# One core of Trainium2, a two-layer hybrid backbone: the last feed-forward by seven half-size products, and four pieces of work moved in the streams before it

## The chip, the cores and the metric

The kernel runs on one core of one Trainium2 chip. The core has a matrix engine (PE, with its weight loads listed apart as PEld), a vector engine (DVE), a scalar engine (ACT), a general one (POOL), and queues that move data between the chip's memory and the core (their issues are listed under SP). Each engine works through its own list of instructions in order and waits there for what others must deliver. The metric is the time of one execution on the device in microseconds (us), and one kernel's time is the median of several runs.

## What is computed

Two layers over 512 latent tokens and 256 context tokens with 1024 features. Each layer is a half-step feed-forward, a mixing step (attention with grouped heads, a short gated convolution, attention with compressed queries and keys), and a second half-step feed-forward. The context leaves the net after the mixing step of the second layer, so the last of the four feed-forwards has 512 tokens and the other three have 768.

```
def rms_norm(x, g):
    xf = x.astype(jnp.float32)
    y = xf * lax.rsqrt(jnp.mean(xf * xf, axis=-1, keepdims=True) + EPS)
    return (y * g.astype(jnp.float32)).astype(x.dtype)

def swiglu(h, wg, wu, wd):
    return (jax.nn.silu(h @ wg) * (h @ wu)) @ wd

def half_ffn(h, g, shift, scale, gate, wg, wu, wd):
    return h + 0.5 * gate * swiglu(modulate(rms_norm(h, g), shift, scale), wg, wu, wd)
...
    for l in range(DEPTH):
        need_ctx = l < DEPTH - 1
        ml = jnp.split(s_lat @ w_mod[l] + b_mod[l], N_MOD, axis=-1)
        ...
        x = half_ffn(x, g_norm[l, 0], ml[0], ml[1], ml[2], ffn_w_gate[l, 0], ffn_w_up[l, 0], ffn_w_down[l, 0])
        ctx = half_ffn(ctx, g_norm[l, 0], mc[0], mc[1], mc[2], ffn_w_gate[l, 0], ffn_w_up[l, 0], ffn_w_down[l, 0])
        ...
        x = x + ml[5] * y_l
        x = half_ffn(x, g_norm[l, 2], ml[6], ml[7], ml[8], ffn_w_gate[l, 1], ffn_w_up[l, 1], ffn_w_down[l, 1])
        if need_ctx:
            ctx = ctx + mc[5] * y_c
            ctx = half_ffn(ctx, g_norm[l, 2], mc[6], mc[7], mc[8], ffn_w_gate[l, 1], ffn_w_up[l, 1], ffn_w_down[l, 1])
    return x
```

The feed-forward's inner width is 2816, which is 22 blocks of 128. Everything is float32.

## The kernel before

**Products.** A float32 product is made of three passes over rounded parts: every operand x is split into a high part (a rounding copy on ACT) and a low part (x minus the high part, on DVE), and PE adds high·high, high·low and low·high (`mm3`). Features lie on the 128 partitions and tokens along the free axis, so an activation is eight tiles `h[k]` of 128 features, each a pair (high, low). A weight block of 128 output features is a tile of 128 x 1024, loaded by SP into one of two buffers `wr` (line 194), rounded by ACT into `wh` and completed by DVE into `wl` (three buffers each).

**Feed-forward (`ffn`, line 598).** `classical(m, ...)` (line 608) makes block m of the inner width: 24 matmuls for the gate weights and 24 for the up weights over all tokens, then Silu on ACT, the product with the up result on DVE, and the split of the activation. The blocks are cut into chunks; after each chunk `residual` multiplies the chunk's activations with the down weights, eight output tiles `o`, and adds the result times a gate to the stream `xT`. The last feed-forward takes the branch at line 648: all 22 blocks classical, in chunks of 8, 7 and 7 (`CHUNKS`, line 25).

The other three feed-forwards have 768 tokens and do only their first chunk (for the very first one, two chunks) that way. For the rest they cut gate and up weights, features and tokens into halves and take a block's gate and up results from seven half-size products in place of eight (a scheme of the Winograd kind). `sums(j)` (line 667) makes four sums of activation halves on DVE and splits them, `sums_late` a fifth, `Weights` (line 718) makes sums of weight halves on DVE, and `Tile` (line 773) issues the seven products `p1` to `p7`, each 4 x 3 matmuls over half of the tokens, by `seventh` (line 762). The loop at line 896 is an order written out by hand: from line 871 on, the instructions of PE, DVE and ACT are chained, so that each engine runs them in program order. For a tile m in the middle of a chunk the stages are as follows; p is tile m-1, nx the weights of tile m+1.

| PE | DVE, in order | ACT, in order | SP |
|---|---|---|---|
| p1 | p.act1, low of split_up | high of split_up, high of tile m-2 | nx gate block into `wr` |
| p2 | low of tile m-2 | take1 | nx up block into `mscr` (one buffer) |
| p6 | gate1 | Silu | |
| p5 | low of nx.split_gate | take2, high of nx.split_gate | |
| p7 | nx.sums (three) | | |
| p.p3 | up2, low of nx.split_sums | take3, high of nx.split_sums | |
| p4 | p.gate2, low of split_fourth, p.act2, nx.fourth | Silu, high of split_fourth | |

`p6`, `p7` and `p4` add into the accumulator that `take1`, `take2` and `take3` read just before. Two `mod_step` calls, after the low of split_up and after gate1, run pieces of the modulation there.

**Modulation.** The 72 rows of scale, shift and gate of each layer are dot products on DVE: one block (l, j, k) is a load of 128 x 1024 and one DVE instruction into `junk` for each stream. They wait in `mod_queue`; `pump(n)` issues n blocks, `pump(upto=...)` all up to a given row. The mixing step's output product is a `residual` with `npump=1` (line 1712), one block after each of five output tiles. In a feed-forward, `pump(upto=gate)` (line 714) issues what is left of the gate row ahead of the first chunk's `residual`.

**`residual` (line 422) with a next stage.** After the last output tiles it also normalizes the stream for the next stage: first the latent tokens (`c0`), then the context tokens, or the second half of the latent ones (`c1`). For c0, the loop over k to line 579 makes tile k (`scaled` on DVE, `high` on ACT, `low` on DVE), multiplies it at once with up to three weight blocks `E` of the next stage (`products`), and fits in the remaining down products of c1 (`run`), their update, square and count. At k == 6 the third block is split where it was not split earlier (line 552), at k == 7 the mean and inverse root of c1 are taken on DVE (line 570) and spread by PE transposes into `R1`. A second loop makes the c1 tiles; in it `wn_late` (line 1191) loads and splits eight token weight blocks, one for each k (`LATE`, line 43).

**`mixing` (line 1200).** Up to line 1566 the chained part projects the compressed queries `cq` and keys; `stats["cq"]` adds up their squares over the features by PE matmuls with a vector of ones (`count_steps`), and these counts stand between the matmuls of the first query tile `uq(0)` (line 1563). `rr["ckv"]`, an inverse root of eight small DVE instructions, is at line 1387. `attend` (line 1137) then runs the attention units; `up_at(0, uq, 1)` puts the second query tile into unit 0.

Of the kernel before, what the change touches and what calls it, by code (L numbers as in the profile page):

```python
# [8 lines left out]
F32 = mybir.dt.float32  # L9
# [33 lines left out]
LATE = {k: 1 for k in range(8)}  # L43
# [4 lines left out]
def tile_net(ctx: ExitStack, tc: tile.TileContext, a, out):  # L48
# [373 lines left out]
    def residual(blocks, rhs, gate, streams, nxt, pre=None, late={}, view=nv, npump=0, ntail=3):  # L422
# [94 lines left out]
        run(4)  # L517
# [27 lines left out]

        for k in range(KD + 1):
# [51 lines left out]
    def ffn(l, f, hin, streams, nxt, pre, npump, late={}):  # L598
# [5 lines left out]
        fast = w == T  # L604
        view = tv if fast else nv
        res = None

        def classical(m, ahead):
# [14 lines left out]
            else:  # L623
                pts = [ps(), ps()]
                for j in range(2):
                    project(full(pts[j]) if fast else plain(pts[j], cols), wgu[j], h)
                parts = [(banks(pts[0]), banks(pts[1]), pairs) if fast else
# [20 lines left out]
        if not fast:  # L648
            for ci, (m0, n) in enumerate(CHUNKS):
                acts = []  # L650
                for m in range(m0, m0 + n):
                    acts.append(classical(m, {}))
                    if m < 18:
                        pump(npump)
                if ci == 0:
                    pump(upto=gate)
                lastc = ci == len(CHUNKS) - 1
                if lastc:
                    before_last()
                res = residual(down(m0, n), acts, gate, streams, nxt if lastc else None, pre, late if lastc else {})  # L660
            return res


        nslow = 2 if i == 0 else 1
        U, V, t1 = [None] * 4, [None] * 2, [None] * 2

        def sums(j):

            X, Y = temp(), temp()
            lo, hi = slice(0, HALF), slice(HALF, T)  # L670
# [1318 lines left out]
```

## Time and profile before

| | |
|---|---|
| Median of 3 runs | 2800.01 us (2799.33 to 2801.71) |
| The profiled execution | 2797.64 us, of which its span is 2795.8 us |
| DVE busy | 1944.1 us, 70% of the span |
| ACT busy | 1089.0 us, 39% |
| POOL busy | 146.9 us, 5% |
| Read from memory | 247.19 MB |
| Mean granted TensorE clock | 0.990 |

The stages follow each other in the span: the first feed-forward to about 570 us, mixing of layer 0 to about 1010, its second feed-forward to about 1550, the third feed-forward to about 2075, mixing of layer 1 to about 2405, and the last feed-forward from about 2430 to the end. In a view by windows a row gives the window, its length, the busy time and the instructions of PE, PEld, DVE, ACT and POOL, the granted clock of PE, and the busy share and rate of the data movers. In a view by order of time a row gives the start, the duration, the engine, the operation with output and inputs, and in brackets how long the engine sat idle before it and what ended that.

### The profile page before, as it was taken

What the parts mean: (1) busy time and instruction counts of PE and PEld (TensorE: products, weight loads), DVE (VectorE), ACT (ScalarE), POOL (GpSimd) and SP (SyncE); (2) the same over time, 40 slices, a digit from 0 to 9 for tenths busy, and PEclk for the clock granted to TensorE, in tenths of its full rate; (3) what the DMA queues carried; (4) which work ended last, traced back from release to release, by engine and by line L of the source; (5) the groups of instructions that cost most, each with busy time, mean ns of one, the idle gap of its engine ahead of it and who ended that gap; (6) DMA issues with size and microseconds to landing.
All of it is one profiled execution on the core that took longest, in us unless ns stands there. A gap on an engine that the chain in (4) does not pass through costs nothing. (4 is left out here: it accounts for less than half of the span.)

```text
span 2795.8 us, 38908 instructions
## 1 busy us (share of the span) xinstructions
PE 2696.0 (96%) x15440; PEld 2515.6 (90%) x15440; DVE 1944.1 (70%) x3293; ACT 1089.0 (39%) x1860; POOL 146.9 (5%) x194
## 2 busy tenths in 40 slices
PE   8999999999889998999999999999999999999999
PEld 5999999988788888999999899999988788888887
DVE  6857777777688866777777777777766798633333
ACT  5223333341478532333334333333342477322221
POOL 0000000001132200000000000000000233000000
PEclk9999999999999999999999999999999999999999
DMA  7313333233000321333333133333225101232332
GB/s 245 121 56 103 106 106 106 83 103 115 29 2 9 106 77 53 98 106 107 107 107 102 50 94 107 109 107 108 86 64 172 32 9 56 90 104 91 91 98 91
DMA packets 95269, 251.80 MB, mean 90 GB/s; under 512 B 11376, under 2 KB 40816, under 8 KB 95088
## 3 DMA queue, kind: packets, MB, share of 16 engines
q1 hardware_dynamic: 95088, 249.33, 28.2%
q8 instruction: 121, 1.98, 0.3%
q14 instruction: 60, 0.49, 0.1%
HBM read 247.19 MB, written 2.10 MB: 89 GB/s over the span
## 5 line engine op out<-in xcount | busy, mean ns | idle before, releaser
L66 PE MATMUL ps<-s,wh 128*128 128x384 f32 (+2 forms) x4724 | 1146.5, 349 | 17.3 <-DVE xT L66 11.9
L66 PEld LDWEIGHTS ps<-s,wh 128*128 128x128 f32 x4724 | 832.7, 188 | 90.2 <-issue 15.1
L66 PE MATMUL ps<-s,wl 128*128 128x384 f32 (+2 forms) x2362 | 707.4, 347 | 0.3 <-DVE wl L66 0.3
L66 PE MATMUL po<-s,wh 128*128 128x384 f32 (+2 forms) x2476 | 643.7, 341 | 2.4 <-ACT t L66 1.7
L66 PEld LDWEIGHTS po<-s,wh 128*128 128x128 f32 x2476 | 447.0, 188 | 15.6 <-ACT t L66 2.7
L66 PEld LDWEIGHTS ps<-s,wl 128*128 128x128 f32 x2362 | 428.7, 188 | 32.7 <-DVE wl L66 0.8
L66 PE MATMUL po<-s,wl 128*128 128x384 f32 (+2 forms) x1238 | 422.2, 341 | 0.3 <-DVE wl L66 0.3
L66 ACT CAST wh<-wr 128x1024 fp32r<-128x1024 f32 (+5 forms) x219 | 209.1, 957 | 449.1 <-PE ps L66 319.1
L66 DVE TENSOR_TENSOR wl<-wr,wh 128x1024 fp32r<-128x1024 f32 (+5 forms) x219 | 243.3, 1113 | 194.1 <-ACT wh L66 191.8
L66 DVE SCALAR_TENSOR_TENSOR xT<-ps,mod,xT 128x256 f32<-128x256 f32 (+1 forms) x392 | 212.6, 585 | 193.8 <-PE ps L66 191.9
L66 DVE SCALAR_TENSOR_TENSOR junk<-mr,sb 128x1024 fp8e4<-128x1024 f32 x224 | 273.4, 1221 | 16.4 <-DMA mr<-in_wm_dram 15.5
L66 PEld LDWEIGHTS po<-s,wl 128*128 128x128 f32 x1238 | 232.2, 188 | 6.7 <-DVE wl L66 0.5
L66 PE MATMUL po<-s,s 128*128 128x256 f32 (+3 forms) x952 | 157.6, 316 | 9.6 <-DVE t L66 3.7
L66 PEld LDWEIGHTS po<-s,s 128*128 128x128 f32 x952 | 140.5, 190 | 17.7 <-ACT s L66 6.5
L66 ACT COPY t<-po 128x384 f32<-128x384 f32 (+1 forms) x161 | 76.9, 478 | 195.2 <-PE po L66 194.2
L66 ACT ACTIVATE t<-t 128x384 f32<-128x384 f32 x106 | 55.7, 526 | 238.2 <-DVE t L66 238.2
L66 DVE TENSOR_TENSOR t<-ps,t 128x384 f32<-128x384 f32 (+3 forms) x91 | 55.3, 608 | 112.3 <-PE ps L66 110.3
L66 DVE TENSOR_TENSOR s<-t,s 128x768 fp32r<-128x768 f32 (+2 forms) x129 | 98.6, 767 | 41.0 <-ACT s L66 40.8
L66 ACT CAST s<-t 128x768 fp32r<-128x768 f32 (+2 forms) x129 | 87.9, 684 | 97.2 <-DVE t L66 96.9
L66 PE MATMUL po<-s,w 128*128 128x384 f32 x636 | 119.7, 336 | 0.0
L66 PE MATMUL po<-ident,t 128*128 128x128 f32 x684 | 101.7, 280 | 13.9 <-ACT t L66 12.9
L66 DVE TENSOR_TENSOR t<-po,t 128x384 f32<-128x384 f32 (+2 forms) x169 | 94.0, 557 | 28.6 <-ACT t L66 28.0
(180 smaller groups left out, 3094.6 us busy)
## 6 DMA issues: line engine op xcount, KB each, us to landing
mr<-in_wm_dram SPq DMA_DIRECT2D x128, 512.0 KB, 3.7
wr<-in_wg_dram SPq DMA_DIRECT2D x88, 512.0 KB, 3.5
wu<-in_wu_dram SPq DMA_DIRECT2D x53, 512.0 KB, 3.6
t<-in_wd_dram SPq DMA_DIRECT2D x56, 384.0 KB, 3.4
wr<-in_wu_dram SPq DMA_DIRECT2D x35, 512.0 KB, 3.5
wr<-in_wiT_dram SPq DMA_DIRECT2D x22, 512.0 KB, 3.5
wr<-in_wd_dram SPq DMA_DIRECT2D x16, 512.0 KB, 3.5
wr<-in_wo_dram SPq DMA_DIRECT2D x14, 512.0 KB, 4.0
```

The source lines that it names most:

```text
L66: f(*args, **kw)
```

## The change

1. **Last feed-forward.** The branch at line 648 goes. The last feed-forward now runs through the same code as the others, with `joint` false, a width `w` of 512 and a half width `hw` of 256: `LAST`, four classical blocks, then three chunks of six tiles by the seven products. The sums of the activations are stored in the free columns of the `h` tiles. The down weights are loaded one output tile at a time (`Down`), and a new loop over eight output tiles stands after each chunk but the last.
2. **`residual`.** Eight units of c1 rather than four run before the first count when `ntail` is 6. In the loop, the third block's high part is made at k == 4 and its low part at k == 5; the counts start at k == 1 and the mean and root are taken at k == 6; `products` moves behind the updates and the counts.
3. **Token weights in pairs.** `wn_late` loads, rounds and splits two blocks of 384 columns at a time, at k = 0, 2, 4 and 6.
4. **Query sums.** The counts of `cq` move from `uq(0)` to `uq(1)` in unit 0 of `attend`, its mean to unit 1; the root of `ckv` moves behind the last square sum of `cq`, and a one-column Exp is added ahead of it.
5. **`npump`** of the mixing step's output product goes from 1 to 2.

```
-CHUNKS = ((0, 8), (8, 7), (15, 7))
+LAST = ((0, 4), (4, 6), (10, 6), (16, 6))
-LATE = {k: 1 for k in range(8)}
+LATE = {0: 1, 2: 1, 4: 1, 6: 1}
...
-        run(4)
+        run(8 if ntail == 6 else 4)
...
+        third = []
         for k in range(KD + 1):
             if k < KD:
                 cur = HMod(h[k], k, c0, R, A[i0][:, k:k + 1], B[i0][:, k:k + 1], hview)
                 cur.scaled()
                 cur.high()
-            if k == 6 and len(E) == 2:
-                E.append(wsplit(raws[2], 1024))
+            if k == 4 and len(E) == 2:
+                third.extend(pool.tile([P, 1024], F32R, name=nm(t), tag=t, bufs=3) for t in ("wh", "wl"))
+                se.copy(third[0], raws[2])
             if prev is not None:
                 prev.low()
-                if k <= hold or k == KD:
-                    products(k - 1)
-            prev = cur
+            if k == 5 and third:
+                ve.tensor_sub(third[1], raws[2], f32(third[0]))
+                E.append(tuple(third))
             second_update()
             second_square()
             run(3)
-            if k == 2:
+            if k == 1:
                 S[1].zero()
                 S[1].count(S[1].acc, False)
-            if k >= 2:
-                for _ in range(2 if k < 7 else len(s1)):
+            if k >= 1:
+                for _ in range(2 if k < 6 else len(s1)):
                     if s1:
                         S[1].count(s1.pop(0), not (s1 or ready or updated or units))
-            if k == 7:
-
+            if k == 6:
                 S[1].mean()
                 r1 = rsqrt(S[1].ms, S[1].w // P)
+            if prev is not None and (k <= hold or k == KD):
+                products(k - 1)
+            prev = cur
+            if k == 7:
+
                 R1 = po()
...
         def sums(j):
...
+            if joint:
+                if j % 2 == 0:
+                    V[j // 2] = slot(F32R), slot(F32R)
+                t3.append(tuple(t[:, c] for t in V[j // 2]))
+                U[j] = slot(F32R), slot(F32R)
+                t4.append(tuple(t[:, lo] for t in U[j]))
+                t2.append(tuple(t[:, hi] for t in U[j]))
+            else:
+
+                if j % 3 == 0:
+                    V[j // 3] = slot(F32R), slot(F32R) if j == 0 else None
+                free = slice(w, w + hw)
+                t3.append(tuple(t[:, hw * j:hw * j + hw] for t in V[0]) if j < 3 else (V[1][0][:, 0:hw], V[1][0][:, hw:w]))
+                t4.append(tuple(t[:, free] for t in h[j]))
+                t2.append(tuple(t[:, free] for t in h[j + 4]))
...
-        chunks = FIRST if i == 0 else FAST
-        sums_at = (2, 3, 4, 5) if i == 0 else (0, 1, 2)
+        chunks = (FIRST if i == 0 else FAST) if joint else LAST
+        sums_at = (2, 3, 4, 5) if i == 0 else (0, 1, 2) if joint else (0, 1, 2, 3)
...
+            if not joint:
+                pts = [ps(), ps()]
+                for o in range(KD):
+                    if o > 1:
+                        pts.append(ps())
+                    if o == 0:
+                        project(whole(pts[0]), D[0].w[0], acts, range(n - 1))
+                        D[1].split()
+                        project(whole(pts[1]), D[1].w[0], acts, range(n - 1))
+                        D.append(Down(2, m0, n))
+                        D.append(Down(3, m0, n))
...
+                    project(whole(pts[o]), D[o].w[0], acts, range(n - 1, n) if o < 2 else None)
+                    update(o, pts[o])
+                    if o == 1:
+                        nt = Tile(nx.m)
+                        nt.p1()
+                        nx.load_up()
+                continue
...
-        k, both = len(wn), slot(F32R)
-        hi, lo = both[:, 0:384], both[:, 384:768]
-        wn.append((hi, lo))
-        raw = wload(a["wiN"][l, k, :, 0:384], 384)
-        se.copy(hi, raw[:, 0:384])
-        return lambda: ve.tensor_sub(lo, raw[:, 0:384], f32(hi))
+        k, hi, lo = len(wn), slot(F32R), slot(F32R)
+        wn.extend((hi[:, c:c + 384], lo[:, c:c + 384]) for c in (0, 384))
+        raw = pool.tile([P, 1024], F32, name=nm("wr"), tag="wr", bufs=NWR)
+        nc.sync.dma_start(out=raw[:, :T].rearrange("p (o c) -> p o c", o=2),
+                          in_=a["wiN"][l, k:k + 2, :, 0:384].rearrange("o p c -> p o c"))
+        se.copy(hi, raw[:, :T])
+        return lambda: ve.tensor_sub(lo, raw[:, :T], f32(hi))
...
-            elif i == 4:
-                rr["ckv"] = rsqrt(stats["ckv"].ms, NT)
...
         stats["cq"].accumulate()
+        se.activation(out=small(1), in_=zeros[:, 0:1], func=AF.Exp)
+        rr["ckv"] = rsqrt(stats["ckv"].ms, NT)
...
-        sums = uq(0, stats["cq"].count_steps(stats["cq"].acc))
-        stats["cq"].mean()
-        sums()
+        uq(0)()
...
-        up_at(0, uq, 1)
+        up_at(0, lambda t: uq(t, stats["cq"].count_steps(stats["cq"].acc)), 1)
         at(0, "end", lambda: uq(2)())
+        at(1, "b", lambda: stats["cq"].mean())
...
-        return residual(lambda o: first_out[0] if o == 0 else wblock(a["wo"][l, o]), rhs, (l, 5), streams, nxt, pre, npump=1)
+        return residual(lambda o: first_out[0] if o == 0 else wblock(a["wo"][l, o]), rhs, (l, 5), streams, nxt, pre, npump=2)
```

More of the change, by code (lines that the diff above doesn't have):

```diff
@@ L647, in ffn @@
         gate = (l, 6 * f + 2)
[L648 to L661, printed above, removed]
         nslow = 2 if i == 0 else 1
         U, V, t1 = [None] * 4, [None] * 2, [None] * 2
+        t2, t3, t4 = [], [], []
         def sums(j):
             X, Y = temp(), temp()
[L670 to L671 removed]
+            lo, hi = slice(0, hw), slice(hw, w)
+            c = slice(hw * (j % 2), hw * (j % 2) + hw)
             if j % 2 == 0:
                 t1[j // 2] = slot()
[L674 to L677 removed]
+            T1 = t1[j // 2][:, c]
+            if joint:
[12 more added lines that the diff above has]
+                t2.append(tuple(t[:, free] for t in h[j + 4]))
+            X, Y = X[:, :w], Y[:, :w]
+            ve.tensor_add(X, f32(h[j][0])[:, :w], f32(h[j][1])[:, :w])
+            ve.tensor_add(Y, f32(h[j + 4][0])[:, :w], f32(h[j + 4][1])[:, :w])
             ve.tensor_sub(T1, X[:, hi], X[:, lo])
@@ L882, in update @@
         def update(o, pt):
+            if not joint:
+                x = tv(xT[o], LAT)
+                ve.scalar_tensor_tensor(out=x, in0=cv(pt, LAT), scalar=mod[gate][0][:, o:o + 1], in1=x, op0=ALU.mult, op1=ALU.add)
+                return
             v = banks(pt)
@@ L972, in ffn @@
                     D[0].split()
-                    D.append(Down(1, m0, n, lastc))
+                    D.append(Down(1, m0, n, lastc or not joint))
                 t.p4()
```

102 lines of the change are left out of this document (55 added, 47 removed).

## The prediction, made before the changed kernel was run

> **What bounds the kernel now.** I read the page's busy times first, then the busy time by windows of 70 us, then, in order of time, every row of PE that waited over 0.4 us, and last DVE and ACT through one tile of the joint feed-forwards and through the end of the last one.
>
> ```profile
> PE 2696.0 (96%) x15440; PEld 2515.6 (90%) x15440; DVE 1944.1 (70%) x3293; ACT 1089.0 (39%) x1860; POOL 146.9 (5%) x194
> ```
> ```profile
> 1050.00:1120.00 70.00, 58.21 (x325) 57.02 (x325) 47.08 (x80) 19.84 (x31) 0.00 (x0) 0.93 0.17 51
> ...
> 1190.00:1260.00 70.00, 69.96 (x402) 69.67 (x402) 55.46 (x89) 23.97 (x36) 0.00 (x0) 1.00 0.34 108
> ...
> 2450.00:2520.00 70.00, 70.00 (x301) 56.40 (x300) 24.56 (x27) 19.55 (x25) 0.00 (x0) 1.00 0.30 91
> ```
>
> The feed-forwards are bound by PE: in 1190 to 1260 (joint, seven products) and 2450 to 2520 (the last one, classical) it has no idle time. But DVE is busy 55 of 70 us in the first and 25 of 70 in the second. What the change puts into the last feed-forward is the method that loads DVE, with shorter products to hide it behind. So there are two questions: which idle times of PE go, and whether PE is still the bound in the last stage.
>
> **Part 1, the last feed-forward.** A classical tile is 48 matmuls of 512 columns. At 70/301 = 0.2326 us each that is 11.16 us. A tile by seven products is 7 x 4 x 3 = 84 matmuls of 256 columns. Their pace is in the rows:
>
> ```profile
> 2439.82 0.28 PE L66 MATMUL ps<-s,wl 128*128 128x256 f32 x1
> ...
> 2442.64 0.28 PE L66 MATMUL ps<-s,wl 128*128 128x256 f32 x1
> ```
>
> Eight groups of three stand between these starts: 2.82/24 = 0.1175 us each, so 9.87 us a tile on PE, 1.29 us less than classical. The weight loads don't forbid it: they keep this pace here. Down products are unchanged (8 x 22 x 3 matmuls of 512 columns in all).
>
> Now DVE. The joint tile in mid-chunk shows its own cycle (384 columns):
>
> ```profile
> 1721.04 0.55 DVE L66 TENSOR_TENSOR t<-po,t 128x384 f32<-128x384 f32 x1
> ...
> 1723.78 0.55 DVE L66 TENSOR_TENSOR t<-ps,t 128x384 f32<-128x384 f32 x1
> ...
> 1726.25 1.23 DVE L66 TENSOR_TENSOR wl<-wr,wh 128x1024 fp32r<-128x1024 f32 x1 [0.77 <-ACT wh L66]
> ...
> 1729.98 1.23 DVE L66 TENSOR_TENSOR wl<-ws,wh 128x1024 fp32r<-128x1024 f32 x1
> 1731.12 0.55 DVE L66 TENSOR_TENSOR t<-po,t 128x384 f32<-128x384 f32 x1
> 1732.77 0.70 DVE L66 TENSOR_TENSOR w<-wr,w 128x512 fp32r<-128x512 f32 x1 [1.10 <-ACT w L66]
> ...
> 1734.45 0.55 DVE L66 TENSOR_TENSOR t<-po,t 128x384 f32<-128x384 f32 x1
> ```
> ```profile
> 1724.37 0.53 ACT L66 ACTIVATE t<-t 128x384 f32<-128x384 f32 x1 [3.79 <-DVE t L66]
> 1724.80 0.46 ACT L66 COPY t<-po 128x384 f32<-128x384 f32 x1
> 1725.16 1.06 ACT L66 CAST wh<-wr 128x1024 fp32r<-128x1024 f32 x1
> ```
>
> From act1 (1721.04) to the next tile's act1 (1734.45) are 13.41 us, and each wait of DVE in it is for ACT, none for PE. The chain goes to and fro: gate1 on DVE (1723.78), Silu, take2 and the cast of the next gate block on ACT, the low part on DVE (1726.25); then the sums, their cast, their low part (1729.98); gate2 (1731.12), Silu and a cast, the low part (1732.77). Both engines run in program order, so these steps cannot slide past each other. With 14.6 us of PE per tile (84 x 70/402) the cycle hides. With 9.87 it doesn't. For 256 columns:
>
> ```profile
> 1722.64 1.22 DVE L66 SCALAR_TENSOR_TENSOR junk<-mr,sb 128x1024 fp8e4<-128x1024 f32 x1
> ...
> 2432.20 0.42 DVE L66 TENSOR_TENSOR t<-po,t 128x256 f32<-128x256 f32 x1 [1.21 <-ACT t L66]
> ...
> 2436.60 0.69 DVE L66 TENSOR_TENSOR s<-t,s 128x512 fp32r<-128x512 f32 x1 [0.69 <-ACT s L66]
> ```
>
> - The modulation step at 1722.64 goes, since its queue is empty by then: -1.14 (1722.64 to 1723.78). The second such step lies inside the wait for ACT and saves nothing.
> - Five operations of 0.55 us become 0.42: -0.65.
> - Two Silu and take2 lie inside the waits, some 0.1 us shorter each (an estimate from 0.55 against 0.42): -0.3.
> - The low part of the activation of tile m-2 is missing in this early tile: +0.6 (0.69 less the overlap of instructions in a row).
>
> 13.41 - 1.14 - 0.65 - 0.3 + 0.6 = 11.92 us per tile, **above** the classical 11.16. By this PE waits some 2 us in each tile, and the stage loses a little. Carrying the three queues through a chunk of six with these durations (each instruction at the later of its engine's turn and its input), tiles start at 0, 6.9, 17.6, 30.2, 42.2 and 54.2 us, and the last product ends at 67.5; the first tile's p1, 1.4 us, lies in the down stage before. 68.9 against 6 x 11.16 = 67.0 is +1.9 a chunk, +5.7 in three.
>
> Edges: the first seven-product tile waits for take1 before p6, +0.5. The last chunk's final activation is ready 4.1 us after its last product, and the first down product needs it after 15 matmuls, 3.5 us: +0.6. The down stage of the four classical tiles is 8 x 12 x 0.2326 = 22.3 us and now holds, beside 8 splits and updates (about 11 us), the last activation sums, the late sum and the first tile's weight sums (about 13 us): I take +1.5, between 0 and 4. The activation sums of the other three tiles, some 4 us of DVE each, lie beside classical tiles where DVE is busy 25 of 70 us: nothing. Part 1: **+8.3 us**; if PE were the bound, 18 x -1.29 + 1.5 = -21.7.
>
> **Parts 2 to 5, idle times of PE that are addressed.**
>
> ```profile
> 593.07 0.40 PE L66 MATMUL po<-ident,m 128*128 128x128 f32 x2 [1.92 <-DVE m L66]
> ...
> 1023.50 1.44 PE L66 MATMUL po<-s,we 128*128 128x512 f32 x5 [0.98 <-DVE s L66]
> 1026.46 0.43 PE L66 MATMUL po<-ident,m 128*128 128x128 f32 x2 [1.53 <-DVE m L66]
> ...
> 1086.52 1.62 PE L66 MATMUL ps<-s,wh 128*128 128x384 f32 x4 [10.25 <-DVE xT L66]
> 1087.94 0.84 PE L66 MATMUL ps<-s,wl 128*128 128x384 f32 x2
> 1088.58 1.48 PE L66 MATMUL ps<-s,wh 128*128 128x384 f32 x4
> ...
> 1565.73 0.40 PE L66 MATMUL po<-ident,m 128*128 128x128 f32 x2 [1.92 <-DVE m L66]
> ...
> 2092.00 0.40 PE L66 MATMUL po<-ident,m 128*128 128x128 f32 x2 [1.92 <-DVE m L66]
> ...
> 2421.08 0.86 PE L66 MATMUL po<-s,we 128*128 128x256 f32 x5 [1.50 <-DVE s L66]
> 2423.61 0.40 PE L66 MATMUL po<-ident,m 128*128 128x128 f32 x2 [1.67 <-DVE m L66]
> ```
>
> *Norm roots and gate blocks.* PE waits for the roots (DVE m) five times: 1.92 x 3 + 1.53 + 1.67 = 8.96 us. The counts now stand before the products, and the root one step earlier, so it is ready while PE still multiplies; late next is R1's own chain, equal before and after. The two waits for DVE s, 0.98 + 1.50, follow the third block's split at k == 6, which moves to k == 4 and 5. Nothing is added but order. 11.4 us, of which I take 9.5; bounds 5 and 14 (the counts may also fill short waits before the first products).
>
> *npump=2.* The 10.25 us: DVE works off what is left of the gate row before it may update `xT`. Six `junk` instructions stand in that stretch, and five blocks of two rows now go earlier, so none is left. The six matmuls after it take 2.06 us (1086.52 to 1088.58), where six of 384 columns take 1.04 (70/402 each), and the window's granted clock is 0.93. The Trainium skill (TensorE: Matmul & The Clock Gate, What's actually happening) has the clock halved after an idle window of about 3.4 us until it has been busy as long; the trace agrees with the factor of two. I take 9.8 of idle time (0.5 stay, like other chunk ends) and 1.2 of slow matmuls: 11.0. The ten instructions, 11.4 us of DVE, go beside the output product, where DVE has waits like
>
> ```profile
> 985.20 1.14 DVE L66 SCALAR_TENSOR_TENSOR xT<-ps,mod,xT 128x512 f32<-128x512 f32 x2 [5.27 <-PE ps L66]
> ```
>
> Their five loads pass SP there too, where the next weight block then comes later: up to 2 us. Bounds 6 and 12.
>
> *Query sums.*
>
> ```profile
> 727.59 1.47 PE L66 MATMUL po<-ident,s 128*128 128x128 f32 x12
> 731.77 0.60 PE L66 MATMUL po<-zeros,ident 128*128 128x12 f32 x2 [2.71 <-DVE k L66]
> 734.14 0.59 PE L66 MATMUL po<-ones,s 128*128 128x2 f32 x2 [1.76 <-DVE s L66]
> ...
> 746.75 0.97 PE L66 MATMUL ps<-k,s 128*128 128x512 f32 x4 [1.43 <-ACT t L66]
> ...
> 2205.52 0.59 PE L66 MATMUL po<-ones,s 128*128 128x2 f32 x2 [4.79 <-DVE s L66]
> ```
>
> The counts wait for the last square sum, and `uq(0)` waits behind them. Without them `uq(0)` needs only the last evacuation and its accumulator, about 1.1 us after the transposes in layer 0 and 1.5 in layer 1. So 2.71 + 1.76 - 1.1 = 3.4 and 4.79 - 1.5 = 3.3 us come back, and the matmuls behind, at half pace there as after the 10.25 us, some 2 us in each layer. The Exp ahead takes the table load out of unit 0 (part of the 1.43); the moved root, eight small DVE instructions or 1.6 us, is now before unit 0's maximum and gives part of that back: 0. In all 10.5; bounds 5 and 15, since attention behind it has its own waits.
>
> *Token weights.*
>
> ```profile
> 2103.81 0.48 DVE L66 SCALAR_TENSOR_TENSOR t<-xT,mod,po 128x256 f32<-128x256 f32 x1
> ...
> 2104.43 5.77 PE L66 MATMUL po<-s,s 128*128 128x384 f32 x24 [3.66 <-DVE t L66]
> ```
>
> In layer 1 PE waits until the chain of c1 tiles, 2092.4 to 2104.3, frees R1's accumulator. Per two tiles it has four operations of 0.40 and, in pairs, one low part of 768 columns, about 0.87: 2.47 us, 9.2 to the last `scaled`, not 11.9. -2.7; bounds -3.7 and 0 if a pair's load lands late. In layer 0 other products cover it: 0.
>
> **Sum:** +8.3 - 9.5 - 11.0 - 10.5 - 2.7 = -25.4. Against the profiled 2797.64 us (span 2795.8) that is 2772.2; the median of the runs is 2.4 higher, so **2774.6**.
>
> **Rivals.**
> - *PE stays the bound in the last stage.* For it: DVE's bare work per tile, some 8.7 us of instructions, is below 9.87; against it: the waits quoted, which ordered queues force. The Trainium skill (Perfetto Trace Analysis, Identifying the Most-Contended Engine) takes the engine of highest occupancy as the one to optimize; by that PE, here at 96% against 70%, would stay the limit. Part 1 is then -21.7: 2744.6.
> - *The idle times move on.* The waits that go are replaced by the next in line (ACT in attention, a load in the output product), so only half of the 33.7 us comes: 2791.
> - *Slower: the up block's load.* It has a single buffer: the load for tile m+1 starts when the low part of split_up(m) is made, and the sums wait for it on DVE.
>
> ```profile
> wu<-in_wu_dram SPq DMA_DIRECT2D x53, 512.0 KB, 3.6
> ```
>
>  From that low part's end to the sums the cycle leaves 3.8 us; each us of landing above it adds one to a tile. At 3.6 it decides nothing. To end slower than before, 18 tiles must each lose 25.4/18 = 1.4 us more, so landing must reach 3.8 + 1.4 = 5.2 us; at 5.8 it would be 2774.6 + 18 x 2.0 = 2810.6.
> - *The change does not do what it says:* if the instructions in the trace keep the old order at the root or the counts, part 2 gives nothing; within the second rival.
>
> **How the numbers follow.** Forecast 0.64; PE stays the bound 0.17; idle times move on 0.12; slower 0.07. 0.2% is 5.6 us, about what a measurement of this kernel can tell from no change. Forecast and PE-bound are faster wholly, of the second rival a little over half: faster 0.88, same 0.05, slower 0.07. The forecast's own range, from the bounds above, is 2762 to 2790. The range that holds 8 in 10 reaches into the PE-bound case: **2743 to 2791**.
>
> **What would show it.** Right: in the last stage tiles 11.5 to 12.5 us apart, PE busy 80 to 85% of a tile, its waits ended by DVE and DVE's by ACT; no wait at the root over 0.5 us; the 10.25 us under 1. Wrong: PE without idle time in the last stage's tiles (then the cycle argument fails), DVE waiting there for `wu` loads, or a new wait of PE over 3 us in the output product of layer 0.

## The result, and the profile after

| | median | range | runs |
|---|---|---|---|
| before | 2799.73 us | 2799.33 to 2801.71 | 4 |
| changed | 2767.6 us | 2762.16 to 2768.58 | 4 |

The ratio is 0.988 with a 95% interval of 0.9863 to 0.9897: faster by 32 us, where 25 were forecast (2774.6, range 2743 to 2791). The profiled execution took 2766.78 us, its span is 2764.9.

The page of the changed kernel, busy times:

```profile
PE 2673.9 (97%) x16088; PEld 2527.6 (91%) x16088; DVE 2061.7 (75%) x3516; ACT 1143.6 (41%) x1989; POOL 147.0 (5%) x194
```

The changed kernel by windows (columns as before): the stretch in which PE had waited 10.25 us, and a mid-chunk stretch of the last feed-forward.

```profile
1050.00:1120.00 70.00, 68.94 (x391) 67.94 (x390) 53.02 (x83) 26.18 (x42) 0.00 (x0) 1.00 0.24 81
2660.00:2730.00 70.00, 62.23 (x480) 59.74 (x479) 49.44 (x78) 32.81 (x58) 0.00 (x0) 0.95 0.26 85
```

The first row answers to 58.21 us and a clock of 0.93: the hole is closed. The second answers to 70.00: in the last feed-forward PE, without idle time before, now stands still for 7.8 of 70 us. Both directions were forecast. In views by order of time `...` stands for rows left out. PE of the changed kernel in order of time:

```profile
592.01 0.38 PE L66 MATMUL po<-ident,m 128*128 128x128 f32 x2
...
726.93 1.46 PE L66 MATMUL ps<-we,s 128*128 128x288 f32 x9 [0.94 <-DVE k L66]
...
1065.10 0.94 PE L66 MATMUL ps<-s,wh 128*128 128x384 f32 x4 [0.49 <-DVE xT L66]
...
1538.33 0.38 PE L66 MATMUL po<-ident,m 128*128 128x128 f32 x2
...
2071.52 8.73 PE L66 MATMUL po<-s,s 128*128 128x384 f32 x49 [1.51 <-DVE t L66]
...
2165.45 1.46 PE L66 MATMUL ps<-we,s 128*128 128x288 f32 x9 [0.82 <-ACT t L66]
...
2379.33 0.40 PE L66 MATMUL po<-ident,m 128*128 128x128 f32 x2 [0.88 <-DVE m L66]
...
2519.48 0.73 PE L66 MATMUL ps<-s,wh 128*128 128x512 f32 x2 [0.86 <-ACT wh L66]
2520.47 0.50 PE L66 MATMUL ps<-s,wl 128*128 128x512 f32 x1 [0.26 <-DVE wl L66]
...
2551.62 0.40 PE L66 MATMUL po<-s,wh 128*128 128x256 f32 x2
...
2656.53 0.39 PE L66 MATMUL po<-s,wh 128*128 128x256 f32 x2
...
2679.72 0.50 PE L66 MATMUL po<-s,wh 128*128 128x256 f32 x2 [2.58 <-ACT t L66]
...
2691.72 0.50 PE L66 MATMUL po<-s,wh 128*128 128x256 f32 x2 [1.88 <-ACT t L66]
...
2703.72 0.50 PE L66 MATMUL po<-s,wh 128*128 128x256 f32 x2 [0.59 <-ACT t L66]
...
2715.72 0.50 PE L66 MATMUL po<-s,wh 128*128 128x256 f32 x2 [1.87 <-ACT t L66]
```

The root's matmuls (`ident,m`) at 592.01 and 1538.33 no longer wait, the 10.25 us are 0.49, the 3.66 of the token weights 1.51. The root of mixing 1 still waits 0.88 us. The four rows at the end are `p6` of successive tiles, waiting for `take1`: tiles are 12.0 us apart there. Over the twelve tiles inside the three chunks (by `gate1`, without the first distance of each chunk) the mean is 12.2 us and the longest 12.8.

Matching row starts of both traces give the lead of the changed kernel at each place, that is, how much earlier it gets there (the `ident,m` rows are the second root of a stage; both transposes rows are `ps<-ident,s`):

| place | before | after | lead | gained since |
|---|---|---|---|---|
| second root, feed-forward 1 | 593.07 | 592.01 | 1.1 | 1.1 |
| query transposes, layer 0 | 726.93 | 723.85 | 3.1 | 2.0 |
| end of the first query tiles | 762.02 | 753.25 | 8.8 | 5.7 |
| second root, mixing 0 | 1026.46 | 1014.93 | 11.5 | 2.8 |
| row that waited for `xT` | 1086.52 | 1065.10 | 21.4 | 9.9 |
| second root, feed-forward 2 | 1565.73 | 1538.33 | 27.4 | 6.0 |
| second root, feed-forward 3 | 2092.00 | 2061.25 | 30.8 | 3.4 |
| query transposes, layer 1 | 2198.70 | 2162.73 | 36.0 | 5.2 |
| last attention transposes | 2365.90 | 2323.03 | 42.9 | 6.9 |
| second root, mixing 1 | 2423.61 | 2379.33 | 44.3 | 1.4 |
| end of the span | 2795.8 | 2764.9 | 30.9 | -13.4 |

So in this pair of traces the other four edits gained 44.3 us, where 33.7 were forecast, and the last feed-forward gave back 13.4, where it was 8.3. Both signs were as forecast, both sizes too small in this pair.

One pair of traces is not the whole record. Eight traces with the four edits (this one and those of `e1`, `e3` and `e8` to `e12` below) reach the second root of mixing 1 between 2377.86 and 2387.08 us, the two without them (the kernel before and `e2`) at 2423.61 and 2416.05. Their gain is thus anything from 29 to 46 us, and 33.7 lies within. Single lines of the table can be off by some us in the same way. The loss in the last feed-forward is firmer: from that root to the end, seven traces with the changed feed-forward in its first order take 384.9 to 388.7 us, and the two with the classical one 372.1 and 372.2, which is 12.7 to 16.6 more.

Why the tile takes 12.0 us: one tile of the changed kernel on DVE, from `gate1` to the next `gate1`.

```profile
2681.33 0.41 DVE L66 TENSOR_TENSOR t<-ps,t 128x256 f32<-128x256 f32 x1
2683.43 1.23 DVE L66 TENSOR_TENSOR wl<-wr,wh 128x1024 fp32r<-128x1024 f32 x1 [1.69 <-ACT wh L66]
...
2687.16 1.23 DVE L66 TENSOR_TENSOR wl<-ws,wh 128x1024 fp32r<-128x1024 f32 x1 [0.24 <-ACT wh L66]
...
2689.72 0.69 DVE L66 TENSOR_TENSOR w<-wr,w 128x512 fp32r<-128x512 f32 x1 [0.99 <-ACT w L66]
...
2693.33 0.42 DVE L66 TENSOR_TENSOR t<-ps,t 128x256 f32<-128x256 f32 x1
```

DVE waits 1.69 + 0.24 + 0.99 = 2.92 us, each time for ACT, and PE waits for `take1` on ACT. No wait of DVE is for PE. The rest, 12.0 - 2.9 = 9.1 us, is DVE's own work. In two of the twelve tiles DVE also waits for a load, the up block's; the first of them is the tile of 12.65 us in the first chunk, in which PE's matmuls run at full pace (10.14 us busy, as in a tile of 12.00):

```profile
2487.03 0.69 DVE L66 TENSOR_TENSOR ws<-wu 128x512 f32<-128x512 f32 x1 [0.55 <-DMA wu<-in_wu_dram]
```

The other wait is 0.38 us, at 2568.14.

### The profile page after: what moved, and what is told of

Read it like the earlier page. It is cut to its first block, busy times and chain, and to the rows that moved or that the text cites. A ratio compares the mean times of both kernels' runs of the same rounds, so it can differ in the third digit from the quotient of the medians.

```text
span 2764.9 us, 40598 instructions
## 1 busy us (share of the span) xinstructions
PE 2673.9 (97%) x16088; PEld 2527.6 (91%) x16088; DVE 2061.7 (75%) x3516; ACT 1143.6 (41%) x1989; POOL 147.0 (5%) x194
## 5 line engine op out<-in xcount | busy, mean ns | idle before, releaser
L66 PE MATMUL ps<-s,wh 128*128 128x384 f32 (+2 forms) x4292 | 988.2, 339 | 8.1 <-ACT t L66 3.8
L66 PE MATMUL po<-s,wh 128*128 128x384 f32 (+2 forms) x3196 | 780.9, 330 | 23.8 <-ACT t L66 22.9
L66 PEld LDWEIGHTS po<-s,wh 128*128 128x128 f32 x3196 | 564.3, 191 | 41.6 <-ACT t L66 27.7
L66 PE MATMUL po<-s,wl 128*128 128x384 f32 (+2 forms) x1598 | 526.2, 329 | 0.0
L66 PEld LDWEIGHTS ps<-s,wl 128*128 128x128 f32 x2146 | 386.7, 188 | 21.4 <-DVE wl L66 2.7
L66 DVE TENSOR_TENSOR wl<-wr,wh 128x1024 fp32r<-128x1024 f32 (+4 forms) x195 | 208.9, 1074 | 137.6 <-ACT wh L66 137.5
L66 DVE SCALAR_TENSOR_TENSOR junk<-mr,sb 128x1024 fp8e4<-128x1024 f32 x224 | 273.1, 1219 | 12.9 <-DMA mr<-in_wm_dram 11.9
L66 ACT CAST wh<-wr 128x1024 fp32r<-128x1024 f32 (+4 forms) x195 | 179.6, 924 | 219.0 <-PE ps L66 144.8
L66 ACT COPY t<-po 128x384 f32<-128x384 f32 (+2 forms) x215 | 96.8, 450 | 220.6 <-PE po L66 219.6
L66 PEld LDWEIGHTS po<-s,s 128*128 128x128 f32 x952 | 139.8, 189 | 12.7 <-DVE pl L66 2.5
L66 PE MATMUL po<-s,w 128*128 128x384 f32 (+1 forms) x852 | 147.6, 322 | 0.0
L66 PEld LDWEIGHTS po<-s,w 128*128 128x128 f32 x852 | 138.1, 188 | 0.0
L66 DVE TENSOR_TENSOR s<-t,s 128x768 fp32r<-128x768 f32 (+3 forms) x144 | 103.9, 725 | 45.1 <-ACT s L66 44.6
```

Of the source, the lines that this page charges most:

```text
L66: f(*args, **kw)
```

## The experiments

Kernels are named by the first part of their label. "The stage" below is the time from the second root of mixing 1 to the end of the span: 372.2 us before (2795.8 - 2423.61), 385.6 after. Ratios are to the kernel before on the same chip, with their 95% intervals.

**Each side of the change alone.** `e1` puts the last feed-forward back, `e2` makes only that edit.

```
e1:  -LAST = ((0, 4), (4, 6), (10, 6), (16, 6))
     +CHUNKS = ((0, 8), (8, 7), (15, 7))          # and ffn() as before the change
e2:  kernel before, with LAST and the changed ffn()
```

> The changed kernel with the last feed-forward put back to 22 classical blocks in chunks of 8, 7 and 7; the four other edits stay. My theory: the seven products cost 8.3 us by the prediction and some 13 us by the two traces (the stage is 44.5 us ahead when it begins and 30.9 at its end), so this kernel takes 2767.6 - 8 to 13 = 2754 to 2759. Rival, PE is the bound of the seven products and they gain 21.7: then 2789, and the four other edits would give only some 11 us.

> The kernel before with the last feed-forward by seven products alone; none of the four other edits. My theory: 2799.7 + 8 to 13 = 2808 to 2813, slower than before. Rival, PE is the bound of the stage: 2799.7 - 21.7 = 2778. If the parts influence each other, the two parts run alone will not add up to the whole: e1 minus before plus e2 minus before should be -32 within 4 us.

Measured: `e1` 2753.7 us, ratio 0.9823 (0.9782 to 0.9863), stage 372.1 us. `e2` 2810.1 us, ratio 1.0027 (1.0009 to 1.0044), stage 387.2 us. The changed feed-forward by itself makes the kernel slower, and the four other edits by themselves are better than the whole. The rival that PE bounds the changed stage falls (2789 and 2778). The two effects add up to -42 us by the ratios, where the whole is -32; that is not within the 4 us expected, but the intervals, some 11 us to either side, hold it, so the runs do not decide whether the parts influence each other. By the stage the changed feed-forward costs 13.5 us (changed kernel against `e1`) and 15.0 (`e2` against the kernel before). The ratio of `e2` shows only 7.6 us (2.5 to 12.3), because its trace reaches the stage 7.6 us earlier than that of the kernel before, with the same code up to there; why stays open.

**The order of ACT and DVE.** `e3` moves one cast, `e8` moves four steps.

```
e3:       t.p4()
     +    t.w.high_fourth()      # ACT: round the fourth block
          p.gate2()              # DVE add, ACT Silu
     -    t.w.split_fourth()     # ACT round, DVE low part
     +    t.w.low_fourth()
e8:  also: take1 ahead of tiles[j-2].high(); tiles[j-2].low() behind gate1's add;
     nx.high_gate() between gate1's add and its Silu
```

> The changed kernel; in the last feed-forward ACT rounds the fourth sum's block before the Silu of p.gate2 and not behind it. Nothing is left out. My theory (tiles are 12.0 us apart because DVE and ACT wait for each other in turn): the 0.99 us that DVE waits there in each of 12 tiles goes, tiles come 11.0 us apart, 2767.6 - 11.9 = 2756. Rival, PE sets the tile: no change. Rival, the load of the next gate or up block sets it: DVE or ACT waits for the load in place of the 0.99, no change.

> As e3, and in the last feed-forward also: take1 ahead of the activation cast of tile m-2 on ACT, the low part of tile m-2 behind gate1 on DVE, the cast of the next gate block ahead of the Silu of gate1. Nothing is left out. My theory: DVE's waits of 1.69 and 0.99 us in a tile shrink to some 0.5 in all, and PE with 9.87 us a tile becomes the bound: 12 tiles x 2.1 = 25 us less, 2742, PE's idle time in 2676 to 2716 of the changed kernel (about 2 us a tile) mostly gone. Rival, the gate block's load (its buffer comes free with the fourth block's low part, 3.3 us to landing) is next: tiles some 11 us apart, 2756, with ACT waiting for wr. Rival, PE was the bound: no change.

Measured: `e3` 2754.6 us (ratio 0.9832, 0.9795 to 0.9869), stage 372.5 us, 13.1 less than the changed kernel. PE of `e3` in order of time, `p6` of the last four tiles:

```profile
2679.20 0.50 PE L66 MATMUL po<-s,wh 128*128 128x256 f32 x2 [2.74 <-ACT t L66]
...
2690.13 0.50 PE L66 MATMUL po<-s,wh 128*128 128x256 f32 x2 [1.12 <-ACT t L66]
...
2701.06 0.50 PE L66 MATMUL po<-s,wh 128*128 128x256 f32 x2 [1.12 <-ACT t L66]
...
2711.99 0.50 PE L66 MATMUL po<-s,wh 128*128 128x256 f32 x2 [1.11 <-ACT t L66]
```

They are 10.93 us apart: a tile is shorter by 1.07, the wait of 0.99 that was taken away and a little more (in the mean of the twelve tiles 11.2 against 12.2). No work was removed and PE's instructions are the same, so it is the order of the two engines that set the tile.

`e8` took 2751.6 us (0.9818, 0.9784 to 0.9851), stage 372.0 us: nothing beyond `e3`, where 14 us more were expected. ACT of `e8` shows why:

```profile
2671.42 1.06 ACT L66 CAST wh<-wr 128x1024 fp32r<-128x1024 f32 x1 [0.92 <-DMA wr<-in_wg_dram]
2672.37 0.41 ACT L66 ACTIVATE t<-t 128x256 f32<-128x256 f32 x1
...
2683.22 1.04 ACT L66 CAST wh<-wr 128x1024 fp32r<-128x1024 f32 x1 [2.78 <-DMA wr<-in_wg_dram]
2684.17 0.41 ACT L66 ACTIVATE t<-t 128x256 f32<-128x256 f32 x1
```

The cast that was put ahead of the Silu now waits for the gate block's load, and the Silu waits behind it. These two casts are 11.8 us apart; the tiles of `e8` vary from 10.0 to 12.0 us and have a mean of 10.9. The rival, which had tiles of some 11 us and ACT waiting for `wr`, holds here: the gate block's load is next in line.

**Another order, with one and with two buffers for the up block.** In `e9` and `e10` the sums of weight halves come ahead of the gate block's low part, so that this load and the casts lie beside DVE's work.

```
     t.p1(); p.act1(); t.w.split_up(); t.take1(); tiles[j-2].high()
     nx.load_up(); nx.load_gate()
     t.p2(); t.p6(); t.gate1(); tiles[j-2].low(); t.p5(); t.take2()
     nx.high_gate(); nx.sums(); nx.low_gate()
     t.p7(); p.p3(); nx.high_sums(); t.take3(); t.up2(); nx.low_sums()
     t.p4(); t.w.high_fourth(); p.gate2(); t.w.low_fourth(); p.act2(); nx.fourth()
e9:  tag="mscr" if joint or self.m % 2 else "mq"    # e10: tag="mscr" always
both: D[1].split() ahead of the last tile's act1, as in e12
```

> The changed kernel with another order in the tiles of the last feed-forward (up block's load first, into two buffers in turn; take1 ahead of the activation cast; gate1 ahead of the low part of tile m-2; weight sums ahead of the gate block's low part; the casts of the gate block, the sums and the fourth block ahead of the copies and the Silu they stood behind) and the second down block split before the last activation. Nothing is left out. My theory: with no wait for ACT or for a load in it, DVE's own work of 8.9 us is the whole cycle and PE's 84 x 0.1175 = 9.87 us is the bound: tiles 9.9 us apart, the stage 14 us shorter than in the kernel with the fourth block first (372.5 us from the last root to the end), so some 2740, and PE without idle time in mid-chunk. Rival, the gate block's load (3.3 to 4.4 us from issue) still ends later than DVE's turn: tiles 10.4 to 11, 2748.

> As the one before, but with the single buffer of the up block. This is the prediction's slower rival in a tighter cycle: the load for tile m+1 starts behind the low part of split_up(m), and the sums need it 0.95 us after that (gate1 0.34, low part of m-2 0.61). My theory: with 3.4 us from issue to landing DVE waits some 2.4 us for wu in each tile, tiles come 11.3 us apart, 12 x 1.4 = 17 us slower than the one before, some 2757. If the load did not decide: the same time as the one before.

Measured: `e9` 2733.0 us, ratio 0.9755 (0.9738 to 0.9772), stage 349.5 us. `e10` 2759.5 us, 0.9849 (0.9833 to 0.9865), stage 373.1 us. `e9` by windows, and `gate1` of three tiles on DVE:

```profile
2650.00:2690.00 40.00, 40.00 (x356) 40.00 (x355) 34.45 (x56) 23.73 (x42) 0.00 (x0) 1.00 0.29 90
```
```profile
2663.04 0.42 DVE L66 TENSOR_TENSOR t<-ps,t 128x256 f32<-128x256 f32 x1 [0.21 <-PE ps L66]
...
2672.56 0.42 DVE L66 TENSOR_TENSOR t<-ps,t 128x256 f32<-128x256 f32 x1 [0.21 <-PE ps L66]
...
2682.08 0.42 DVE L66 TENSOR_TENSOR t<-ps,t 128x256 f32<-128x256 f32 x1 [0.21 <-PE ps L66]
```

PE has no idle time, and `gate1` waits for PE and not the other way round: PE is the bound. Tiles are 9.52 us apart here, and 9.9 in the first chunk, where PE has no idle time either. The stage is 22.7 us shorter than the classical one, against the 21.7 that the prediction gave for "PE stays the bound". DVE of `e10`, the first of the three sums:

```profile
2679.70 0.69 DVE L66 TENSOR_TENSOR ws<-wu 128x512 f32<-128x512 f32 x1 [2.46 <-DMA wu<-in_wu_dram]
...
2691.01 0.69 DVE L66 TENSOR_TENSOR ws<-wu 128x512 f32<-128x512 f32 x1 [2.41 <-DMA wu<-in_wu_dram]
...
2702.24 0.69 DVE L66 TENSOR_TENSOR ws<-wu 128x512 f32<-128x512 f32 x1 [2.35 <-DMA wu<-in_wu_dram]
```

With one buffer DVE waits 2.4 us for the up block in each tile, and tiles are 11.3 us apart, as worked out (11.5 in the mean of the twelve); the stage is 23.6 us longer than `e9`'s, where 17 were expected, since the tiles of `e9` are 9.35 us apart in the mean and not 9.9. This is the prediction's slower rival in action, in a tighter cycle.

**One other edit undone at a time,** and the changed kernel itself once more.

```
e4:  -npump=2   +npump=1
e5:  counts of cq back in uq(0), the mean behind them, the ckv root at its old place, no Exp ahead
e6:  residual() as before the change
e7:  -LATE = {0: 1, 2: 1, 4: 1, 6: 1}   +LATE = {k: 1 for k in range(8)}   # and wn_late() as before
e11: the changed kernel, unchanged
```

> The changed kernel with npump back at 1 in the mixing step's output product. My theory: the gate row is not worked off when the first down stage of the next feed-forward ends, PE waits some 10 us for xT there again and six matmuls run at half pace: 11 us slower than the changed kernel by the prediction (11.6 by the two traces), so 2779. Rival, the idle times only move on: the earlier blocks cost as much in the output product, 2768 to 2772.

> The changed kernel with the counts of cq back in the first query tile, its mean behind them, the root of ckv at its old place and no Exp ahead. My theory: 10.5 us slower than the changed kernel by the prediction, 12.7 by the two traces (5.7 in layer 0, 7.0 in layer 1), so 2778 to 2780, with PE's waits of 2.71, 1.76 and 4.79 us back. Rival, attention behind it has its own waits and takes half of it: 2773.

> The changed kernel with the old order in residual (four units before the counts, the third block split at k == 6, counts and root late, products ahead of them). My theory: 9.5 us slower by the prediction; by the two traces the five places are 1.5, 3.0, 4.2, 3.4 and 1.3 us apart, 13.4 in all, so 2777 to 2781, with the waits of 1.92 (three times), 1.53 and 1.67 us back. Rival, the waits for the roots are replaced by those for R1's own chain: 2770.

> The changed kernel with the eight token weight blocks loaded and split one by one. My theory: 2.7 us slower by the prediction, all of it in layer 1; by the two traces 3.5 there (the wait of 1.51 becomes 3.66, and matmuls behind it at half pace), and perhaps up to 2 in layer 0, where PE is also 2 us nearer between the residual and the queries: 2770 to 2773. Rival, other products cover it: no change.

> The changed kernel itself, unchanged, so that the kernels with one part undone can be set against it on one chip: 2768 to 2770, ratio 0.988. Its last stage from the last root to the end should take 386 us again, tiles 12.0 us apart.

`e11`: 2770.4 us, ratio 0.9891 (0.9875 to 0.9908), stage 388.7 us, 3.1 more than in the first trace of the same kernel; tiles are 12.0 to 12.6 us apart. `e11` ran on another chip than `e4` to `e7`, so only the ratios, each to the kernel before on its own chip, can be set against each other. In the table the loss is the ratio less 0.9891, times 2800 us; its interval is some 6 us to either side.

| undone | median | ratio | loss | by the two traces | forecast |
|---|---|---|---|---|---|
| `npump` (e4) | 2780.6 | 0.9932 (0.9915 to 0.9948) | 11.5 | 11.7 | 11.0 |
| query sums (e5) | 2783.0 | 0.9936 (0.9917 to 0.9956) | 12.6 | 12.6 | 10.5 |
| roots, gate blocks (e6) | 2786.8 | 0.9955 (0.9943 to 0.9967) | 17.9 | 12.9 | 9.5 |
| token weights (e7) | 2771.1 | 0.9899 (0.9884 to 0.9913) | 2.2 | 7.2 | 2.7 |

The fifth column adds the places of the table of leads: 9.9 and 1.8 of the 6.0 for `npump` (a later row, 1109.95 before and 1086.72 after, has a lead of 23.2), 5.7 + 6.9 for the sums, 1.1 + 2.8 + 4.2 + 3.4 + 1.4 for the roots, 2.0 + 5.2 for the token weights. With its interval the loss for the token weights is not clear of nothing, and 9.5 for the roots is below what `e6` allows. The waits came back where they were: PE of `e4`,

```profile
1070.66 1.62 PE L66 MATMUL ps<-s,wh 128*128 128x384 f32 x4 [10.29 <-DVE xT L66]
```

PE of `e5`,

```profile
734.34 0.59 PE L66 MATMUL po<-ones,s 128*128 128x2 f32 x2 [1.98 <-DVE s L66]
...
2177.14 0.58 PE L66 MATMUL po<-ones,s 128*128 128x2 f32 x2 [4.78 <-DVE s L66]
```

PE of `e6`,

```profile
1531.76 0.51 PE L66 MATMUL ps<-s,wh 128*128 128x256 f32 x2 [0.58 <-DVE xT L66]
...
1551.83 0.40 PE L66 MATMUL po<-ident,m 128*128 128x128 f32 x2 [1.92 <-DVE m L66]
...
2077.15 0.40 PE L66 MATMUL po<-ident,m 128*128 128x128 f32 x2 [1.91 <-DVE m L66]
2087.43 12.89 PE L66 MATMUL po<-s,s 128*128 128x384 f32 x73 [1.51 <-DVE t L66]
```

and PE of `e7`:

```profile
2080.31 18.30 PE L66 MATMUL po<-s,s 128*128 128x384 f32 x96 [7.17 <-DVE t L66]
```

The last one was not expected. With single weights the wait is 3.66 us in the kernel before, but 7.17 in `e7`, where the root's wait ahead of it is gone: PE comes earlier to a chain on DVE that is no earlier. Here idle time did move on, by 3.5 us, and only the pairs take it away (1.51 in `e6` and in the changed kernel). Parts 2 and 3 depend on each other at this place, so single undoings cannot share out its gain.

**One step at the chunk's end.**

```
e12:  p.low()
     +if not (joint or lastc): D[1].split()
      t.act1()
      ...
     -D[1].split()              # in the loop over o
```

> The changed kernel with one step moved: in the first two chunks of six the second down block is split ahead of the last tile's final products on DVE and ACT, not behind them. Nothing is left out. The prediction gave these chunk ends 1.9 us each and the trace 4.5 and more (a first tile's p6 comes 105.2 and 104.9 us after the one before, where 102.4 were predicted). My theory: 1.1 of the missing 2.6 us is PE's two waits for that block (0.86 for wh, 0.26 for wl); they go, the period becomes 103.8, the whole 2.2 us less. Rival, the wait moves to the last activation: the waits are then for s and the period stays at 105.

Measured: 2769.9 us (2 runs; ratio 0.9883, 0.9819 to 0.9947), no difference that can be told. In the trace the two waits are gone. PE of `e12`, `p6` of the first tile of the second and third chunk:

```profile
2550.53 0.40 PE L66 MATMUL po<-s,wh 128*128 128x256 f32 x2
...
2653.70 0.40 PE L66 MATMUL po<-s,wh 128*128 128x256 f32 x2
```

With 2445.66 for the first chunk the periods are 104.9 and 103.2 us, against 105.2 and 104.9 in the changed kernel (from 2446.45, 2551.62 and 2656.53). The down stages inside them, from the first down product (at 2515.57 and 2618.70) to these rows, take 34.96 and 35.00 us, against 36.65 and 36.61: 1.65 us less each, more than the 1.1 of the waits, and PE does not wait for the last activation instead. The tiles hide it in the first chunk: from its first `p6` to its first down product `e12` needs 69.9 us, the changed kernel 68.5, with waits of 0.51 and 0.61 us of DVE for `wu` at 2462.54 and 2487.86.

## Why the prediction held, point by point

- **What bounds the last stage: right, and shown.** Forecast: tiles 11.5 to 12.5 us apart, worked out 11.92, PE's waits ended by the other two engines, DVE's by ACT. Measured: 12.0 where nothing else intervenes, 12.2 in the mean, and `e3` shows the cause by moving one cast. PE was to be 80 to 85% busy in a tile: with a wait of 1.87 in the 12.00 us from 2703.72 to 2715.72 it is 84%. That holds for every other tile; in the tiles between, a stretch at half pace fills PE's wait, and it is busy 95 to 97% (11.40 us of the 12.00 from 2692 to 2704, at a granted clock of 0.86). The window's 62.23/70 = 89% mixes the two and reaches into the down stage.
- **Part 1, size: too small, 8.3 against 13.4.** Two terms of it are measured in the trace, the third is what is left. *The chunk of six:* 67.5 us were carried by hand from `p6` of the first tile to the end of the last product; it takes 68.5, 68.3 and 69.3 (the down products start at 2514.97, 2619.92 and 2725.84), so +9.4 over classical in three chunks, not +5.7. The round trip itself was right, but single tiles are longer, for reasons that were read from rows and not tested: in the tile of 12.65 us DVE waits 0.55 for the up block's load; in the next, of 12.23 us, in which PE runs at half pace for a while, DVE's wait for the gate block's cast is 1.91 and not 1.69. *The down stage after a chunk* was put at nothing beyond its products (8 x 18 matmuls of 0.2326 us) and `p1`, 33.5 + 1.4 us; of the ends of the chunks of six, "Edges" counts the last one only. It takes 36.65 and 36.6, +3.5 in two. This is the step that failed: the second down block is split behind the whole last activation on both engines, and PE waits for it (0.86 + 0.26 at 2519.48). `e12` shows it: with the split ahead of that activation the down stages take 34.96 and 35.00 us, so that the whole excess goes and not only the 1.1 of the waits. *The edges,* put at 2.6, are what is left: 13.4 - 9.4 - 3.5, some 0.5.
- **Roots and gate blocks: sign right, too small, 9.5 against 13 to 18.** Four of the five waits for a root went; in mixing 1, 0.88 of 1.67 us stays, over the 0.5 that the prediction allowed. Of the two waits for `s`, 0.98 went and 0.58 of 1.50 stays. What went adds up to 10.0 us. What the sum left out lies behind a wait in this trace. PE of the kernel before, ahead of the second feed-forward's root:

```profile
1544.08 0.76 PE L66 MATMUL ps<-s,wh 128*128 128x256 f32 x2 [0.58 <-DVE xT L66]
1544.64 0.41 PE L66 MATMUL ps<-s,wl 128*128 128x256 f32 x1
1544.86 0.63 PE L66 MATMUL ps<-s,wh 128*128 128x256 f32 x2
...
1548.08 0.28 PE L66 MATMUL ps<-s,wl 128*128 128x256 f32 x1
```

  This short wait for `xT` went too, since eight units now run ahead of the counts, and with it 3.3 us of matmuls at half pace behind it, to 1547.41 (0.64 us from one group of three to the next, 0.34 at full pace): 1.92 + 0.58 + half of 3.3 is 4.1, and 4.2 were gained at this place. But the half pace belongs to this execution and not to the wait: in `e6` the wait of 0.58 came back at 1531.76 with full pace behind it (0.34 us from one group to the next). It stands six times in the traces of the kernel before, `e2` and `e6`, and half pace follows in two of them. So 10.0 us, and 11.1 with two such waits, are accounted for; the rest of the 13 to 18 stays open.
- **`npump`: right in mechanism and size,** 11.0 against 11.5 and 11.7. The output product of layer 0 got no new wait over 3 us.
- **Query sums: right, a little small,** 10.5 against 12.6. The row behind the transposes waits 0.94 and 0.82 us, forecast 1.1 and 1.5; layer 1 gives 6.9, not 5.3, since the matmuls behind its wait ran at half pace longer than was charged: 7.7 us (2205.5 to 2213.2, granted clock 0.50), of which half, 3.8 and not 2, came back. In layer 0 a stretch of 3.5 us at a clock of 0.53 is left in the changed kernel (733.2 to 736.7).
- **Token weights: the wait right, the account not separable.** 3.66 became 1.51, forecast 0.96. The place gained 5.2 us with the matmuls behind it, and layer 0, put at nothing, 2.0 (which may be chance: for that stretch the kernel before takes 133.9 us, the changed kernel 131.8, but `e1` and `e11` with the same code 133.2 and 132.8); but by `e7` the pairs mostly keep what part 2 would have lost again.
- **Rivals.** *PE stays the bound* did not happen in this change; PE waits in each tile. The Trainium skill (Perfetto Trace Analysis, Identifying the Most-Contended Engine) would have one optimize the engine of highest occupancy; the same section warns that for PE the busy time of matmuls is not a good measure and names, among others, that of the weight loads. PE is the highest by both, 96% and 90%, so by that rule fewer products should have helped. The measurement decides against that reading, until `e9` has taken the waits between the two less busy engines away. *Idle times move on* was true at one place, the token weights. *The up block's load* was put at nothing; in the changed kernel DVE waits for it in two tiles, 0.55 and 0.38 us, and in `e10` 2.4 us a tile.

In the two traces the change is 5.5 us better than its sum (30.9 against 25.4), and not 16 off, because the two misses, 10.6 too little gain and 5.1 too little loss, pull against each other. That the median, 2767.6, came within 7 us of the forecast of 2774.6 is in part luck.

## What to carry to other kernels

An engine that is 50 of 70 us busy can be the bound, if it and a second one hand work to and fro in a fixed order: add up one round trip, waits included, and compare it with the busy engine's share before making that share smaller. When the round trip is too long, move the cast or the copy that nobody needs early behind the one that is awaited, and then look at once for the load that comes next: the order here was worth 13 us of the stage with one step, and 36 with the rest and a second buffer for one block, which made the changed feed-forward better than the classical one (ratio 0.9755, 0.9738 to 0.9772, against 0.9823, 0.9782 to 0.9863). A wait on PE can cost more than its length, since the matmuls behind it may run at half pace, and a wait taken away can reappear where the next chain is no earlier than before.

## What was not expected of the hardware

- **Half pace after some short waits.** PE of the changed kernel in a tile of the last feed-forward:

```profile
2691.72 0.50 PE L66 MATMUL po<-s,wh 128*128 128x256 f32 x2 [1.88 <-ACT t L66]
2692.05 0.28 PE L66 MATMUL po<-s,wl 128*128 128x256 f32 x1
...
2693.45 0.41 PE L66 MATMUL po<-s,wl 128*128 128x256 f32 x1
...
2695.37 0.41 PE L66 MATMUL po<-s,wl 128*128 128x256 f32 x1
...
2696.39 0.28 PE L66 MATMUL po<-s,wl 128*128 128x256 f32 x1
```

  The slow stretch begins 1.1 us after a wait of 1.88 us has ended and lasts some 3.2 us (2692.81 to 2696.01); the granted clock from 2693 to 2696 is 0.50. The Trainium skill (TensorE: Matmul & The Clock Gate, What's actually happening) has a window of about 3.4 us; the length agrees, the idle time before it is shorter than such a window. In this tile it costs nothing: the next `p6` waits 0.59 instead of 1.88 us, and the tile is 12.00 us long all the same. Not every such wait is followed by it: behind the 2.58 us at 2679.72 the clock stays at 1.00 (2680 to 2692). No run here tells what decides.
- **Two paces at full clock.** Products of 256 columns take 0.1175 us each in the rows of the prediction and 9.52/84 = 0.1133 in the last chunks of `e9`, both with a granted clock of 1.00. In the first chunk of `e9`, with tiles 9.9 us apart, they take 0.118, at 1.00 too. No run here tells what sets the one or the other.
- **One kernel's executions differ in stages that no edit touches.** `e2` reached the last stage at 2416.05, the kernel before at 2423.61, with the same code up to there. Differences of a few us are therefore read from one stage here, not from two totals; and even the last stage took 385.6 and 388.7 us in two traces of the changed kernel.
